# A fixed TensorE order and one head pipeline in the first layer's two attentions of a diffusion backbone

## The chip, the cores and the metric

One core of a Trainium2 chip runs the whole program. The metric is device time in microseconds (us) of one execution; less is better. PE is TensorE, DVE VectorE, ACT ScalarE, POOL GpSimd, SP SyncE; L234 is line 234 of the kernel. All data is float32.

## The reference, cut to what matters

Two layers over 512 latent and 256 context tokens of width 1024. The change touches the first sub-layer of layer 0 alone; the rest (its expert MoE, then layer 1) stays as it is.

```python
mods = split(silu(c) @ ada_w[l] + ada_b[l], 6)          # also for c_ctx: shift, scale, gate, twice
h  = rms_norm(x, norm_mix[l]) * (1 + sc1) + sh1         # hc the same from ctx
aq, ak, av, nq, nk, nv = split_cols(h @ w_in, 6 * [512])
# differential attention, 4 heads of 2 x 64: rope on aq and ak of the latents
p = softmax(q[c] . k[c] / 8)                            # c = 0, 1; keys: latents, then context
a = rms_norm((p[0] - lam * p[1]) @ v, subln) * (1 - lam_init)
# neighbourhood attention, 8 heads of 64: a window of 8 x 16 latents with a bias, and all context
nb = softmax([q . k_win / 8 + rpb, q . k_ctx / 8]) @ [v_win, v_ctx]
y = concat([a, nb]) @ w_out                             # context tokens: the same among themselves
x = x + g1 * y                                          # then the MoE of layer 0
```

## The kernel before

The kernel is written against a tile framework: it traces instructions in program order, derives all waits itself, and a scheduler then chooses each engine's order by when it takes an instruction's inputs and buffers to be ready. Only what is traced through the class Pinned (L168) keeps its place: each such TensorE instruction is tied behind the TensorE instruction traced just before it. Before the change only the MoE of layer 0 uses it.

`mix0` (L395) first makes the first third of layer 0's modulation (`ada_first`) and the normalized, transposed input `hh`, `hl` (a high and a low part, so that a product is three matmuls: `mm3`, L321). Then come twenty projection jobs (list `jobs`): per differential head a query and a key of 128 columns, two value jobs of 256, and the same for four pairs of neighbourhood heads. `proj_t` (L474) makes a query or key: 24 matmuls with 512 columns into `ps_px`, 24 with 256 into `ps_pc`; differential ones are rotated on ACT, DVE and POOL (L484 to L488). `proj_v` (L499) makes values: six groups of 24 matmuls with 256 columns, `ps_pv`. `ada` (L217) makes one of five remaining modulation vector groups: eight weight blocks of 1 MB each through two buffers, loaded by SP (L221), four 32-column matmuls per block (each is two instructions) into `ps_ada`, then transposes `ps_adat` (L244). `px`, `pc`, `pv`, `ps_ada` and `ps_adat` share two PSUM buffers.

Jobs and modulation are generators. `dense(n)` puts n jobs into the queue `fill`; `ada` generators go into `fill2`. `run_fill(n)` (L612) takes n steps of `fill` (up to the next yield), and every third turn goes to `fill2` in between; `drain` runs what is left of `fill`. A step is three or six projection matmuls, or one modulation block.

`diff_head` (L651) has six units of 128 query rows (four latent, two context). A unit is A: scores `ps_s` of both halves (64 rows of the array each, `mm3p`, L329), maximum, exponential and difference; B: up to six transposes through the single bank `ps_tr` (L687); C: the product with the values, `ps_o` (L697). `weave` (L632) runs A of a unit, then B and C of the unit before, with fill steps between, and ends each head by itself. After the last C of a head comes a chain over POOL, DVE and ACT (L703 to L710) that normalizes `au`; `tail` (L712) transposes it, called by `run_late`. `na_pair` (L734) does the same for two neighbourhood heads, scores `ps_n`, with a lag of two units; POOL adds bias and mask (L753) for DVE's L764, and the scaling is L771. During the last pair no projection is left; `last` feeds pieces of `split_wout` (L342) instead, which cast the output weights on ACT and subtract on POOL or DVE (L356). The output projection, the routing and the MoE follow.

Of the kernel before, what the change touches and what calls it, by code (L numbers as in the profile page):

```python
# [24 lines left out]
EPS = 1e-6  # L25
# [102 lines left out]

def _build(tc, a, out, dump=None, upto=99):
    nc = tc.nc  # L130
    V, S, G, T, Y = nc.vector, nc.scalar, nc.gpsimd, nc.tensor, nc.sync
    P = 128
    if dump is None:
        dump = lambda name, ap: None
# [1 line left out]
    with ExitStack() as root:  # L136
# [32 lines left out]
        class Pinned:  # L169

            @staticmethod
            def matmul(*args, **kw):
                return tc.keep_in_program_order(T.matmul(*args, **kw))  # L173

            @staticmethod
            def transpose(*args, **kw):
                return tc.keep_in_program_order(T.transpose(*args, **kw))  # L177

        garow = [dram.tile([2, 2, D], F32, name=f"garow{l}", tag=f"garow{l}") for l in range(2)]

# [36 lines left out]
        def ada(l, g, csil, wp, pp, sm):  # L217

            def load(k):
                w = wp.tile([P, 2048], F32, name="w_ada", tag="w")  # L220
                Y.dma_start(w, a["ada_w"][l, k * P:(k + 1) * P, g * 2048:(g + 1) * 2048])  # L221
                return w

            br = wp.tile([P, 512], F32, name="adab", tag="br", bufs=1)
            bsrc = a["ada_b"][l:l + 1, g * 2048:(g + 1) * 2048]
            S.dma_start(br, bass.AP(bsrc.tensor, bsrc.offset, [[512, 4], [0, 32], [1, 512]]))
            depth = 2
            ws = deque(load(k) for k in range(depth))
            yield
            ps = pp.tile([P, 512], F32, name="ps_ada", tag="mm")  # L230
            for k in range(8):
                w = ws.popleft()
                for j in range(4):
                    T.matmul(ps[32 * j:32 * j + 32, :], csil[:, k, :], w[:, j * 512:(j + 1) * 512], start=(k == 0), stop=(k == 7))  # L234
                if k + depth < 8:
                    ws.append(load(k + depth))
                yield
            row = sm.tile([P, 512], F32, name="mrow", tag="t2k", bufs=T2K)
            V.tensor_tensor(row, ps, br, op=OP.add)
            yield  # L240
            yield
            pt = pp.tile([P, 4, P], F32, name="ps_adat", tag="mm")
            for c4 in range(4):
                T.transpose(pt[:, c4, :], row[:, c4 * P:(c4 + 1) * P], ident)  # L244
            for c4 in range(4):
                src = pt[:, c4, :].rearrange("p (jh jl q) -> p jh jl q", jh=2, jl=2)[:, :, :, 0:2]
                dst = modT[l][:, 2 * g:2 * g + 2, :, c4::4].rearrange("p m v jl -> p m jl v")
                V.tensor_copy(dst, src)
            for s in range(2):
                if 1 + 3 * s in (2 * g, 2 * g + 1):  # L250
                    for v in range(2):
                        V.scalar_tensor_tensor(Asc[l][s][:, v, :], modT[l][:, 1 + 3 * s, v, :], 1.0, norm_t[:, 2 * s + l, :], op0=OP.add, op1=OP.mult)
            if g:
                for half in range(2):
                    j = 2 * (g - 1) + half
                    G.dma_start(garow[l][g - 1, :, half * 512:(half + 1) * 512], row[32 * j:32 * j + 2, :])
# [138 lines left out]
        def mix0(st, st_h, wu, stage):  # L395
# [78 lines left out]
            def proj_t(wt, dst, scale, rope):  # L474
# [2 lines left out]
                px = pp.tile([P, 512], F32, name="ps_px", tag="mm")  # L477
                for k in range(8):
                    mm3(px, wh[:, k], wl[:, k], hh[:, k, 0:512], hl[:, k, 0:512], k == 0, k == 7)
                    yield  # L480
                if rope is not None:
                    raw = sm.tile([P, 512], F32, name="raw", tag="t2k", bufs=T2K)
                    sh = sm.tile([P, 512], F32, name="sh", tag="t2k", bufs=T2K)
# [8 lines left out]
                pc = pp.tile([P, 256], F32, name="ps_pc", tag="mm")  # L492
                for k in range(8):
                    mm3(pc, wh[:, k], wl[:, k], hh[:, k, 512:768], hl[:, k, 512:768], k == 0, k == 7)
                    if k % 2:
                        yield
                split_ps(dst[:, 0, 512:768], dst[:, 1, 512:768], pc, scale)

            def proj_v(wt, dst, u):  # L499
                wh, wl = wt  # L500
                for i in range(6):
                    pv = pp.tile([P, 256], F32, name="ps_pv", tag="mm")
                    t = slice(i * P, (i + 1) * P)
                    for k in range(8):
                        mm3(pv, hh[:, k, t], hl[:, k, t], wh[:, k, :], wl[:, k, :], k == 0, k == 7)
                        if k % 2:
                            yield
                    if i % 2:
                        S.copy(dst[:, i, 256 * u:256 * u + 256], pv)
                    else:  # L510
                        V.tensor_copy(dst[:, i, 256 * u:256 * u + 256], pv)
# [30 lines left out]
            with tc.tile_pool(name="p0d", bufs=2, reuse_waits="tile") as dp:  # L542
                rope = dp.tile([P, 2, LX], F32, name="rope0", tag="rope0", bufs=1)
                with after[0], after[1], after[2]:
                    Y.dma_start(rope, a["rope0"])
                    prep(1)
                rope_of["r"] = rope
                dense(4)
                drain()
                for h in range(4):  # L550
                    dense(2)
                    for g in (((0, 1),), ((0, 2),), ((1, 0),), ((1, 1), (1, 2)))[h]:
                        fill2.append(ada(*g, csil, aw, pp, sm))
                    diff_head(h, qk["q", "d", h], qk["k", "d", h], vv, nlam, cT, pp, sm, dp)
                    drain()
                    run_late()
            for g in range(3):
                dump(f"caT{g}", cT[g][:, 0])


            dense(2)
            drain(True)
            st_a.close()
            np_ = st.enter_context(tc.tile_pool(name="p0n", bufs=2, reuse_waits="tile"))
            nv = nvt["nv"]
# [8 lines left out]
                G.memset(b[:, :, 256:512], 0.0)  # L574
            cnt = [0]

            def pair(hp):
                na_pair(hp, qk["q", "n", hp], qk["k", "n", hp], nv, nvs, bt, cnt, namask, cT, pp, sm, np_)
                drain()

            for hp in range(3):
                dense(2)
                pair(hp)

            def last(extra):
                def later():
# [2 lines left out]
                    yield from extra  # L589
                fill.append(later())  # L590
                pair(3)
                drain(True)
                for g in range(3):
                    dump(f"cnT{g}", cT[g][:, 1])
                return cT
# [36 lines left out]
        def weave(units, n_a, n_b, n_c, lag=1):  # L632

            late = deque()
            for u in list(units) + [None] * lag:
# [4 lines left out]
                if len(late) > lag:  # L640
# [4 lines left out]
                    prev[2]()  # L645
                    run_fill(n_c)

        def tr_bank(pp):
            return pp.tile([P, 4, P], F32, name="ps_tr", tag="tr", bufs=1)

        def diff_head(h, q, kk, vv, nlam, cT, pp, sm, dp):  # L651
            au = dp.tile([P, 6, P], F32, name="au", tag="au", bufs=1)
            st = dp.tile([P, 6, 8], F32, name="dst", tag="dst")

            def unit(i):
# [6 lines left out]
                def A():  # L662
                    pr = []
                    pss = [pp.tile([P, 1024], F32, name="ps_s", tag="S") for _ in range(2)]
                    for n0 in range(0, nk, 512):
                        n1 = min(n0 + 512, nk)
                        if n0:
                            run_fill(1)
                        mm3p([(pss[c][:, n0:n1], q[r, 0, qs], q[r, 1, qs], kk[r, 0, k0 + n0:k0 + n1], kk[r, 1, k0 + n0:k0 + n1]) for c, r in enumerate(HALF)])
                    for c, ps in enumerate(pss):  # L670
                        V.tensor_reduce(st[:, i, c:c + 1], ps[:, :nk], op=OP.max, axis=AX.X, negate=True)
# [4 lines left out]
                    V.scalar_tensor_tensor(st[:, i, 5:6], st[:, i, 4:5], st[:, i, 2:3], nlam[:, 3:4], op0=OP.mult, op1=OP.mult)  # L676
                    V.scalar_tensor_tensor(pr[0][:, :nk], pr[1][:, :nk], st[:, i, 5:6], pr[0][:, :nk], op0=OP.mult, op1=OP.add)
                    d["p"] = pr[0]
                    d["at"] = dp.tile([P, 6, P], F32, name="at", tag="at")

                def B(g0):
                    g1 = min(g0 + 4, n)

                    def f():
                        pt = tr_bank(pp)
                        for c in range(g0, g1):
                            T.transpose(pt[:, c - g0, :], d["p"][:, c * P:(c + 1) * P], ident)  # L687
# [4 lines left out]
                    return f  # L692

                def C():
                    po = pp.tile([P, P], F32, name="ps_o", tag="pv", bufs=1)
                    for c in range(n):
                        T.matmul(po, d["at"][:, c, :], vv[:, k0 // P + c, h * P:(h + 1) * P], start=(c == 0), stop=(c == n - 1))  # L697
                    S.copy(au[:, i, :], po)
                return A, [B(g0) for g0 in range(0, n, 4)], C

            weave([unit(i) for i in range(6)], 1, 1, 1)
            aj = dp.tile([P, 6, P], F32, name="aj", tag="at")
            G.tensor_tensor(aj, au, au, op=OP.mult)  # L703
            V.tensor_reduce(st[:, :, 6], aj, op=OP.add, axis=AX.X)

            V.scalar_tensor_tensor(st[:, :, 7], st[:, :, 2], EPS, st[:, :, 2], op0=OP.mult, op1=OP.mult)
            V.scalar_tensor_tensor(st[:, :, 6], st[:, :, 6], 1.0 / P, st[:, :, 7], op0=OP.mult, op1=OP.add)
            S.activation(st[:, :, 6], st[:, :, 6], AF.Sqrt)
            V.reciprocal(st[:, :, 6], st[:, :, 6])
            G.tensor_tensor(au, au, st[:, :, 6].unsqueeze(2).to_broadcast([P, 6, P]), op=OP.mult)  # L710

            def tail():  # L712
                yield
                for g0, g1 in ((0, 4), (4, 6)):
                    pt = tr_bank(pp)
                    for i in range(g0, g1):
                        T.transpose(pt[:, i - g0, :], au[:, i, :], ident)
                    for g in range(g0 // 2, g1 // 2):
                        V.tensor_scalar(cT[g][:, 0, h, :], pt[:, 2 * g - g0:2 * g - g0 + 2, :].rearrange("p a b -> p (a b)"), subln, None, op0=OP.mult)
                    yield  # L720
            late.append(tail())

        late = deque()

# [9 lines left out]
        def na_pair(hp, q, kk, nv, nvs, bt, cnt, namask, cT, pp, sm, np_):  # L734
# [70 lines left out]
                        S.copy(cT[2][:, 1, hp, :], po)  # L805
                return A, [B(0), B(1)], C

            weave([unit(i) for i in range(6)], 2, 1, 0, NA_LAG)

        def make_route_tiles(l):  # L810
            if l == 0:
# [997 lines left out]
```

## Time and profile before

| | |
|---|---|
| median of 3 runs | 2063.86 us (2062.2 to 2067.67) |
| the profiled execution | 2060.33 us |
| its span, first to last instruction | 2058.5 us |
| mean granted TensorE clock | 0.979 |
| PE busy | 1868.0 us (91%) |

Around the span lie 1.83 us. Busy time is the union of an engine's instructions. Matmuls are pipelined and their ends modelled, so a busy PE may still run at less than its pace; the distance from one start to the next tells what a matmul holds. Form `128*32` means a matmul with 128 rows and 32 columns of the array. The stages of the page: 0 to 69 us modulation and input, 69 to 335 differential heads, 335 to 522 neighbourhood heads, 522 to 627 output and routing, then MoE, layer 1, MoE.

### The profile page before, as it was taken

What the parts mean: (1) busy time and instruction counts of PE and PEld (TensorE: products, weight loads), DVE (VectorE), ACT (ScalarE), POOL (GpSimd) and SP (SyncE); (2) the same over time, 40 slices, a digit from 0 to 9 for tenths busy, and PEclk for the clock granted to TensorE, in tenths of its full rate; (3) what the DMA queues carried; (4) which work ended last, traced back from release to release, by engine and by line L of the source; (5) the groups of instructions that cost most, each with busy time, mean ns of one, the idle gap of its engine ahead of it and who ended that gap; (6) DMA issues with size and microseconds to landing.
All of it is one profiled execution on the core that took longest, in us unless ns stands there. A gap on an engine that the chain in (4) does not pass through costs nothing.

```text
span 2058.5 us, 25961 instructions
## 1 busy us (share of the span) xinstructions
PE 1868.0 (91%) x10612; PEld 984.2 (48%) x10612; DVE 777.8 (38%) x1703; ACT 462.3 (22%) x880; POOL 244.3 (12%) x216
## 2 busy tenths in 40 slices
PE   5899999997988999999999999999995988788787
PEld 1765556876772333333333389555582323232232
DVE  2445453456463222232313463466653112121023
ACT  3233332344330000000000242355421000000002
POOL 1201111212331000000000020101230000000000
PEclk9999999999998999999999999999997999999999
DMA  9354556213658899999999832200159999999996
GB/s 269 114 189 161 169 171 234 80 57 103 204 200 312 318 385 397 384 397 383 395 388 403 269 90 62 113 1 21 51 202 346 409 409 409 409 409 409 409 409 256
DMA packets 176463, 535.04 MB, mean 260 GB/s; under 512 B 11561, under 2 KB 51817, under 8 KB 171225
## 3 DMA queue, kind: packets, MB, share of 16 engines
q1 hardware_dynamic: 162304, 488.28, 62.8%
q0 software_dynamic: 9296, 32.68, 5.5%
q10 hardware_dynamic: 4744, 12.44, 1.9%
q8 instruction: 83, 1.36, 0.3%
q14 instruction: 36, 0.29, 0.0%
HBM read 515.76 MB, written 16.81 MB: 259 GB/s over the span
## 4 chain that ended last, share of the span: by engine, by line
PE 65%; DMA 23%; DVE 6%; ACT 2%; POOL 2%; issue 2%; SPq 0%; ACTq 0%; POOLq 0%; DVEq 0%
DMA moe_w<-in_moe_w 20%; PE ps_c L173 6%; PE ps_d L173 6%; PE ps_b L173 6%; PE ps_a L173 6%; PE ps_ada L234 3%; PE ps_px L323 3%; PE ps_px L324 2%; PE ps_px L325 2%; PE ps_e L173 2%; PE ps_s L1761 2%; PE ps_y L323 2%; PE ps_y L325 1%; PE ps_y L324 1%; PE ps_o L1784 1%
## 5 line engine op out<-in xcount | busy, mean ns | idle before, releaser
L173 PE MATMUL ps_b<-moe_w,xeT 128*64 128x512 f32 x1024 | 273.4, 597 | 31.4 <-DMA moe_w<-in_moe_w 31.4
L173 PE MATMUL ps_a<-moe_w,xeT 128*64 128x512 f32 x1024 | 275.2, 599 | 2.3 <-DMA moe_w<-in_moe_w 1.1
L173 PE MATMUL ps_d<-moe_w,hidT 128*64 128x512 f32 x1024 | 239.8, 599 | 35.5 <-DMA moe_w<-in_moe_w 35.2
L173 PEld LDWEIGHTS ps_d<-moe_w,hidT 128*64 128x64 f32 x1024 | 76.6, 137 | 193.7 <-issue 128.6
L1128 DVE TENSOR_TENSOR hid<-hid,ps_b 128x512 f32<-128x512 f32 x32 | 22.0, 687 | 379.3 <-PE ps_b L173 362.6
L173 PEld LDWEIGHTS ps_b<-moe_w,xeT 128*64 128x64 f32 x1024 | 76.1, 137 | 185.2 <-issue 131.4
L173 PEld LDWEIGHTS ps_a<-moe_w,xeT 128*64 128x64 f32 x1024 | 74.8, 137 | 135.0 <-issue 117.6
L1127 ACT ACTIVATE hid<-ps_a 128x512 f32<-128x512 f32 x32 | 19.1, 597 | 462.4 <-PE ps_a L173 462.4
L173 PE MATMUL ps_c<-moe_w,xeT 128*32 128x512 f32 x1024 | 113.2, 594 | 0.0
L1137 ACT COPY hidT<-ps_t 128x512 f32<-128x512 f32 x32 | 18.7, 586 | 313.7 <-PE ps_t L177 313.7
L1184 DVE TENSOR_SCALAR xeT<-ps_x,asc,modT 128x64 f32<-128x64 f32 (+1 forms) x256 | 64.4, 319 | 17.3 <-PE ps_x L177 16.5
L323 PE MATMUL ps_y<-woh,ch 128*128 128x512 f32 x160 | 66.0, 413 | 3.1 <-ACT ch L861 3.1
L325 PE MATMUL ps_y<-woh,cl 128*128 128x512 f32 x160 | 64.2, 401 | 0.7 <-POOL cl L862 0.7
L173 PEld LDWEIGHTS ps_c<-moe_w,xeT 128*32 128x32 f32 x1024 | 31.6, 110 | 69.0 <-issue 67.2
L324 PE MATMUL ps_y<-wol,ch 128*128 128x512 f32 x160 | 63.8, 399 | 0.0
L234 PE MATMUL ps_ada<-w_ada,csil 128*32 128x512 f32 x320 | 63.2, 604 | 0.0
L1205 DVE SCALAR_TENSOR_TENSOR ye<-ps_d,gate,g 64x512 f32<-64x512 f32 x32 | 24.0, 749 | 100.9 <-PE ps_d L173 100.6
L323 PE MATMUL ps_px<-hh,wu 128*128 128x512 f32 x128 | 58.0, 453 | 2.3 <-DVE hh L461 1.9
L1172 POOL DMA_INDIRECT xe<-gsrc,gidx x16 | 16.0, 1000 | 365.1 <-PE ps_x L177 348.2
L1333 DVE SCALAR_TENSOR_TENSOR ye<-ps_d,gate,g 128x512 f32<-128x512 f32 x14 | 10.5, 750 | 128.9 <-PE ps_d L173 128.2
L173 PE MATMUL ps_e<-moe_w,hidTc 128*32 128x512 f32 x512 | 57.9, 592 | 1.4 <-DVE yc L1216 1.4
L323 PE MATMUL ps_pv<-wh,hh 128*128 128x256 f32 x192 | 54.8, 285 | 4.6 <-DVE qk_k L319 2.3
(460 smaller groups left out, 3335.1 us busy)
## 6 DMA issues: line engine op xcount, KB each, us to landing
moe_w<-in_moe_w SPq DMA_DIRECT2D x372, 1024.0 KB
w_ada<-in_ada_w SPq DMA_DIRECT2D x40, 1024.0 KB
w_in<-in_even_w_in SPq DMA_DIRECT2D x24, 512.0 KB
w_ada<-in_ada_w SPq DMA_DIRECT2D x16, 512.0 KB
moe_w<-in_moe_w SPq DMA_DIRECT2D x16, 512.0 KB
w_in<-in_odd_w_in SPq DMA_DIRECT2D x15, 512.0 KB
w_out<-in_even_w_out SPq DMA_DIRECT2D x4, 1024.0 KB
gsrc<-xh POOLq DMA_DIRECT2D x8, 512.0 KB, 6.7
```

The source lines that it names most:

```text
L173: return tc.keep_in_program_order(T.matmul(*args, **kw))
L234: T.matmul(ps[32 * j:32 * j + 32, :], csil[:, k, :], w[:, j * 512:(j + 1) * 512], start=(k == 0), stop=(k == 7))
L323: T.matmul(ps, lh, rh, start=first, stop=False)
L324: T.matmul(ps, lh, rl, start=False, stop=False)
L325: T.matmul(ps, ll, rh, start=False, stop=last)
L1127: S.activation(hid, pa, AF.Silu)
L1128: V.tensor_tensor(hid, hid, pb, op=OP.mult)
L1137: S.copy(hT.rearrange("p (h c) t -> p c h t", h=2), pt)
L1184: V.tensor_scalar(xt[:, k, n0:n1], pt[:, c, n0:n1], Asc[0][1][:, v, k:k + 1], modT[0][:, 3, v, k:k + 1], op0=OP.mult, op1=OP.add)
L1205: V.scalar_tensor_tensor(self.ye[0:64, hs], pd[x, :], rt["gate"][x, self.e:self.e + 1], rt["g2"][x, 0, :], op0=OP.mult, op1=OP.mult)
L1761: T.matmul(ps[:, n0:n1], q[e][:, i * P:(i + 1) * P], kk[e][:, n0:n1], start=True, stop=True)
L1784: T.matmul(po[64 * e:64 * e + 64, i * P:(i + 1) * P], mv[:, c, h * 64:h * 64 + 64], d["at"][:, 6 * e + c, :], start=(c == 0), stop=(c == 5))
```

## The change

A class T takes the place of the engine's name; with T.pin set it goes through Pinned. It is set from the first projection job to the end of the last pair. All five modulation groups are queued ahead of the first four jobs. Steps are twice as long (two modulation blocks, six or twelve matmuls). Heads hand their units to one pipeline (class Pipe), which goes on from head to head; the fill step within A is gone; `au` and `at` are allocated later; a head's `tail` runs ahead of the third unit of the next head, the last head's after the values of the neighbourhood heads.

```diff
+        class T:
+            pin = False
+            @staticmethod
+            def matmul(*args, **kw):
+                return (Pinned if T.pin else nc.tensor).matmul(*args, **kw)
...
@@ ada
                 if k + depth < 8:
                     ws.append(load(k + depth))
-                yield
+                if k % 2:
+                    yield
@@ proj_t (the second product and proj_v: k % 2 becomes k % 4 == 3)
                     mm3(px, wh[:, k], wl[:, k], hh[:, k, 0:512], hl[:, k, 0:512], k == 0, k == 7)
-                    yield
+                    if k % 2:
+                        yield
@@ mix0
+                T.pin = True
+                for g in ((0, 1), (0, 2), (1, 0), (1, 1), (1, 2)):
+                    fill2.append(ada(*g, csil, aw, pp, sm))
                 dense(4)
                 drain()
+                pipe = Pipe(1, 2)
                 for h in range(4):
                     dense(2)
-                    for g in (((0, 1),), ((0, 2),), ((1, 0),), ((1, 1), (1, 2)))[h]:
-                        fill2.append(ada(*g, csil, aw, pp, sm))
-                    diff_head(h, qk["q", "d", h], qk["k", "d", h], vv, nlam, cT, pp, sm, dp)
+                    for i, u in enumerate(diff_head(h, qk["q", "d", h], qk["k", "d", h], vv, nlam, cT, pp, sm, dp)):
+                        if i == 2:
+                            run_late()
+                        pipe.push(u, 1, 1)
                     drain()
-                    run_late()
+                pipe.flush(0, 0)
...
             dense(2)
             drain(True)
+            run_late()
...
+            pipe = Pipe(2, 3)
             def pair(hp):
-                na_pair(hp, qk["q", "n", hp], qk["k", "n", hp], nv, nvs, bt, cnt, namask, cT, pp, sm, np_)
-                drain()
+                for u in na_pair(hp, qk["q", "n", hp], qk["k", "n", hp], nv, nvs, bt, cnt, namask, cT, pp, sm, np_):
+                    pipe.push(u, 0, 2)
             for hp in range(3):
                 dense(2)
                 pair(hp)
+                drain()
...
                 pair(3)
+                pipe.flush(0, 2)
                 drain(True)
+                T.pin = False
...
+        class Pipe:
+            def __init__(self, lag_b, lag_c):
+                self.lags, self.units = (lag_b, lag_c), []
+            def push(self, u, n_a, n_c):
+                self.units.append(u)
+                if u is not None:
+                    u[0]()
+                run_fill(n_a)
+                b, c = (self.units[-1 - n] if len(self.units) > n else None for n in self.lags)
+                if b is not None:
+                    b[1][0]()
+                if c is not None:
+                    c[2]()
+                if b is not None:
+                    for x in b[1][1:]:
+                        x()
+                run_fill(n_c)
+            def flush(self, n_a, n_c):
+                for _ in range(self.lags[1]):
+                    self.push(None, n_a, n_c)
@@ diff_head, A
                     for n0 in range(0, nk, 512):
                         n1 = min(n0 + 512, nk)
-                        if n0:
-                            run_fill(1)
...
-            weave([unit(i) for i in range(6)], 1, 1, 1)
+            return [unit(i) for i in range(6)]
@@ na_pair
-            weave([unit(i) for i in range(6)], 2, 1, 0, NA_LAG)
+            return [unit(i) for i in range(6)]
```

## Rows read from the trace of the kernel before

**Rows 1.** The page: engines, and the chain that ended last, by line.
```profile
PE 1868.0 (91%) x10612; PEld 984.2 (48%) x10612; DVE 777.8 (38%) x1703; ACT 462.3 (22%) x880; POOL 244.3 (12%) x216
...
DMA moe_w<-in_moe_w 20%; PE ps_c L173 6%; PE ps_d L173 6%; PE ps_b L173 6%; PE ps_a L173 6%; PE ps_ada L234 3%; PE ps_px L323 3%; PE ps_px L324 2%; PE ps_px L325 2%; PE ps_e L173 2%; PE ps_s L1761 2%; PE ps_y L323 2%; PE ps_y L325 1%; PE ps_y L324 1%; PE ps_o L1784 1%
```
**Rows 2.** Stretches: length, busy PE, PEld, DVE, ACT, POOL; granted clock, DMA share, GB/s.
```profile
69.30:117.40 48.10, 45.55 (x356) 43.02 (x354) 17.18 (x23) 11.75 (x20) 6.52 (x4) 1.00 0.23 67
117.40:335.00 217.60, 210.76 (x1255) 129.37 (x1251) 116.60 (x234) 79.77 (x177) 29.76 (x25) 0.98 0.55 182
...
384.20:488.50 104.30, 103.98 (x806) 81.30 (x804) 55.91 (x134) 40.75 (x102) 11.77 (x10) 1.00 0.15 49
488.50:522.40 33.90, 20.81 (x183) 14.59 (x181) 23.87 (x49) 16.64 (x37) 12.59 (x9) 0.90 0.36 124
```
**Rows 3.** PE in order of time: start, length, what, count; two stretches.
```profile
118.51 0.39 PE L324 MATMUL ps_px<-hl,wu 128*128 128x512 f32 x1
118.74 0.40 PE L325 MATMUL ps_px<-hh,wu 128*128 128x512 f32 x1
119.07 1.06 PE L234 MATMUL ps_ada<-w_ada,csil 128*32 128x512 f32 x8
120.06 0.50 PE L323 MATMUL ps_px<-hh,wu 128*128 128x512 f32 x1
120.40 0.39 PE L324 MATMUL ps_px<-hl,wu 128*128 128x512 f32 x1
...
121.66 1.04 PE L234 MATMUL ps_ada<-w_ada,csil 128*32 128x512 f32 x2
122.64 1.32 PE L333 MATMUL ps_s<-qk_k,qk_q 64*128 64x512 f32 x12
123.89 0.66 PE L687 MATMUL ps_tr<-ident,dp 128*128 128x128 f32 x4
...
331.86 1.90 PE L234 MATMUL ps_ada<-w_ada,csil 128*32 128x512 f32 x10
333.70 0.71 PE L697 MATMUL ps_o<-vv,at 128*128 128x128 f32 x4
```
**Rows 4.** DMA over two stretches (columns as rows 2); the one load within was issued at 175.50.
```profile
175.50 0.33 SPq L221 DMA_DIRECT2D w_ada<-in_ada_w  x1
...
177.00:179.80 2.80, 2.80 (x15) 1.52 (x15) 1.48 (x5) 0.81 (x2) 0.18 (x1) 1.00 0.80 331
179.80:181.50 1.70, 1.70 (x11) 0.79 (x11) 0.66 (x1) 0.00 (x0) 0.00 (x0) 1.00 0.00 0
```
**Rows 5.** The chain behind the first head's last unit, in order of time.
```profile
168.41 0.27 ACT L698 COPY au<-ps_o 128x128 f32<-128x128 f32 x1 [1.22 <-PE ps_o L697]
...
175.69 1.48 POOL L710 TENSOR_TENSOR au<-au,dst 128x768 f32<-128x768 f32 x1 [5.47 <-DVE dst L709]
178.66 0.88 DVE L719 TENSOR_SCALAR cT<-ps_tr,subln 128x256 f32<-128x256 f32 x2 [1.28 <-PE ps_tr L717]
```
**Rows 6.** PE waits: at a head's end, at the first value job; in total (engine <- releaser: us, times, longest).
```profile
163.75 0.68 PE L697 MATMUL ps_o<-vv,at 128*128 128x128 f32 x4 [1.83 <-DVE dst L706]
164.78 0.41 PE L325 MATMUL ps_pc<-hh,wu 128*128 128x256 f32 x1
165.00 0.41 PE L323 MATMUL ps_pc<-hh,wu 128*128 128x256 f32 x1
...
83.94 0.38 PE L323 MATMUL ps_pv<-wh,hh 128*128 128x256 f32 x1 [2.27 <-DVE qk_k L319]
...
PE ps_o L697 <- DVE dst L706: 5.5, 3, 1.8
```
**Rows 7.** DVE, then POOL, in the last pair, in order of time.
```profile
495.95 4.86 DVE L771 TENSOR_SCALAR nsp<-nsp,nst 128x512 f32<-128x512 f32 x2
501.41 0.87 DVE L771 TENSOR_SCALAR nsp<-nsp,nst 128x512 f32<-128x512 f32 x2
...
495.52 5.01 POOL L356 TENSOR_TENSOR wol<-w_out,woh 128x1024 fp32r<-128x1024 f32 x2
```

More of the change, by code (lines that the diff above doesn't have):

```diff
@@ L130, in _build @@
     nc = tc.nc
-    V, S, G, T, Y = nc.vector, nc.scalar, nc.gpsimd, nc.tensor, nc.sync
+    V, S, G, Y = nc.vector, nc.scalar, nc.gpsimd, nc.sync
     P = 128
@@ L172, in matmul, with transpose @@
             def matmul(*args, **kw):
-                return tc.keep_in_program_order(T.matmul(*args, **kw))
+                return tc.keep_in_program_order(nc.tensor.matmul(*args, **kw))
             @staticmethod
             def transpose(*args, **kw):
-                return tc.keep_in_program_order(T.transpose(*args, **kw))
+                return tc.keep_in_program_order(nc.tensor.transpose(*args, **kw))
+        class T:
[3 more added lines that the diff above has]
+                return (Pinned if T.pin else nc.tensor).matmul(*args, **kw)
+            @staticmethod
+            def transpose(*args, **kw):
+                return (Pinned if T.pin else nc.tensor).transpose(*args, **kw)
         garow = [dram.tile([2, 2, D], F32, name=f"garow{l}", tag=f"garow{l}") for l in range(2)]
@@ L494, in proj_t @@
                     mm3(pc, wh[:, k], wl[:, k], hh[:, k, 512:768], hl[:, k, 512:768], k == 0, k == 7)
-                    if k % 2:
+                    if k % 4 == 3:
                         yield
@@ L505, in proj_v @@
                         mm3(pv, hh[:, k, t], hl[:, k, t], wh[:, k, :], wl[:, k, :], k == 0, k == 7)
-                        if k % 2:
+                        if k % 4 == 3:
                             yield
@@ L651, in diff_head @@
         def diff_head(h, q, kk, vv, nlam, cT, pp, sm, dp):
-            au = dp.tile([P, 6, P], F32, name="au", tag="au", bufs=1)
+            au = []
             st = dp.tile([P, 6, 8], F32, name="dst", tag="dst")
@@ L678, in A @@
                     d["p"] = pr[0]
-                    d["at"] = dp.tile([P, 6, P], F32, name="at", tag="at")
                 def B(g0):
@@ L684, in f @@
                     def f():
+                        if g0 == 0:
+                            d["at"] = dp.tile([P, 6, P], F32, name="at", tag="at")
                         pt = tr_bank(pp)
@@ L694, in C @@
                 def C():
+                    if i == 0:
+                        au.append(dp.tile([P, 6, P], F32, name="au", tag="au", bufs=1))
                     po = pp.tile([P, P], F32, name="ps_o", tag="pv", bufs=1)
@@ L697, in C, with post @@
                         T.matmul(po, d["at"][:, c, :], vv[:, k0 // P + c, h * P:(h + 1) * P], start=(c == 0), stop=(c == n - 1))
-                    S.copy(au[:, i, :], po)
+                    S.copy(au[0][:, i, :], po)
+                    if i == 5:
+                        post()
                 return A, [B(g0) for g0 in range(0, n, 4)], C
-            weave([unit(i) for i in range(6)], 1, 1, 1)
[L702 to L710, printed above, removed]
+            def post():
+                aj = dp.tile([P, 6, P], F32, name="aj", tag="at")
+                G.tensor_tensor(aj, au[0], au[0], op=OP.mult)
+                V.tensor_reduce(st[:, :, 6], aj, op=OP.add, axis=AX.X)
+                V.scalar_tensor_tensor(st[:, :, 7], st[:, :, 2], EPS, st[:, :, 2], op0=OP.mult, op1=OP.mult)
+                V.scalar_tensor_tensor(st[:, :, 6], st[:, :, 6], 1.0 / P, st[:, :, 7], op0=OP.mult, op1=OP.add)
+                S.activation(st[:, :, 6], st[:, :, 6], AF.Sqrt)
+                V.reciprocal(st[:, :, 6], st[:, :, 6])
+                G.tensor_tensor(au[0], au[0], st[:, :, 6].unsqueeze(2).to_broadcast([P, 6, P]), op=OP.mult)
+                late.append(tail())
             def tail():
@@ L716, in tail @@
                     for i in range(g0, g1):
-                        T.transpose(pt[:, i - g0, :], au[:, i, :], ident)
+                        T.transpose(pt[:, i - g0, :], au[0][:, i, :], ident)
                     for g in range(g0 // 2, g1 // 2):
@@ L720, in tail @@
                     yield
-            late.append(tail())
+            return [unit(i) for i in range(6)]
         late = deque()
```

## The prediction

> **What bounds the kernel now.** I read the page first: PE is busy 91% of the span and no other engine half of it; the chain that ended last names PE's lines and, with 20%, transfers of the MoE's weights [rows 1]. Those are issued as the MoE frees their buffers, behind the routing, which follows the last pair; so what the touched stretches gain or lose should reach the end one for one. Next the stretches [rows 2]. While heads run, PE is busy 210.76 of 217.60 us; in pairs 0 to 2 103.98 of 104.30. Waits are small there, and a gain must come from shorter PE work. In the last pair PE is busy 20.81 of 33.90, DVE 23.87, the clock .90: nothing is full, and order decides. So I read PE's own order, by the distance from one start to the next, and what one change of work costs [rows 3]; then DMA [rows 4], the end of a head [rows 5], PE's waits [rows 6], the last pair's DVE and POOL [rows 7].
>
> **Longer modulation runs.** A run of eight `ps_ada` instructions holds PE .99 (119.07 to 120.06), one of two .98 (121.66 to 122.64), one of ten 1.84 (331.86 to 333.70) [rows 3]: a block streams once through its column groups for about .85, and a run of two pays as much as one of eight. The 40 blocks stand in 59 runs, since the scheduler cuts blocks up. Pinned, they stand in 20 runs of 16, each 1.85 by the run of ten: 59 x .985 - 20 x 1.85 = 21 less. Going into a run costs .10 (118.74 to 119.07 is .33; between plain matmuls, 118.51 to 118.74, .23), leaving it .10 (120.06 to 120.40 is .34): 39 x .20 = 8 less. Together **-29**.
>
> **Scores in one piece.** A latent unit's two 512-column products are now split by a fill step or by whatever the scheduler found. Unsplit, twelve instructions hold 1.25 (122.64 to 123.89 [rows 3]); a context unit is .55 by the same reading. Counted over the heads, `ps_s` holds 35.5 in 44 runs; in 24 whole ones 16 x 1.25 + 8 x .55 = 24.4. That is -11, and 20 changes of form less at .20, -4: **-15**.
>
> **Waits that go.** With the order fixed and lags of one and two units, C no longer follows its own B, and the value job stands behind other projection. PE's wait at the heads' last C, 5.5 in three [rows 6], goes, with the 2.27 at the first value job [rows 6]. [...] **-10**.
>
> **Waits that come, loads.** The five modulation groups are queued ahead of the first four jobs: 36 steps there bring 18 modulation turns, by my count 11 runs, 8 of them not the first of their group. In program order nothing else can go ahead of a run whose weights are not there. A load issued at 175.50 landed at 179.8, where DMA falls from .80 to 0.00 [rows 4]: 4.3; a second behind it takes some 2.5 more, as 331 GB/s at a share of .80 is about 414 when full, 1 MB. Both buffers come free as the two blocks before end, .9 apart, so the loads land about 3.4 and 5.9 after a run's end; in between stand two projection steps, 2.8. So the next run waits .6, works one block, and waits 1.5 more: 2.0 x 8 = **+16**. Bounds: 0, as the stretch now moves 67 GB/s at a DMA share of .23 [rows 2], and 4.5 x 8 = 36, if `w_in` gets between. What queues behind the waiting PE: the job's steps, then their ACT and DVE work; on SP the next modulation load waits for PE's blocks and holds the `w_in` loads traced behind it, the way from 2.0 to 4.5. Later runs have longer turns between them and wait for nothing. The biases (ACT's queue) and the vector's 4 KB bounce (POOL's queue) move ahead too, at nothing: both queues idle there.
>
> **Waits that come, tails.** Behind a head's last C stands a chain from `au`'s copy, 168.41, to the end of POOL's scaling, 175.69 + 1.48 = 177.17 [rows 5]: 8.8. Before, PE went on with projection. Now `tail` has a fixed place ahead of the next head's third unit, and between C and it stand two transposes (.2), a projection step (1.4) and on average half a modulation run (1.0): 8.8 - 2.6 = 6.2, thrice: **+18.6** (bounds 3 and 8.8 each). Its second half needs the single bank `ps_tr`, freed by two scalings of .44 with what lies around them [rows 5]: 1.1 x 4 = **+4.4**. The last head's first half is covered by value jobs. Behind the waiting PE stands A of the third unit, so the DVE and ACT work of the next units comes later by the same, nothing extra. **Clock:** after such a wait I expect what 163.75 shows, 2 each, for two of the three: **+4**. **Head starts:** the first scores of a head need the key's rotation (ACT, DVE, POOL) in program order behind its last matmul; before, other work went ahead. About 1 for three heads, **+3** (bounds 0 and 2.27 each [rows 6]).
>
> Heads and their projection: -29 - 15 - 10 + 16 + 23 + 4 + 3 = **-8**.
>
> **Pairs 0 to 2** (104.30): 52 runs of other forms become 36, both ways .3 by the price above: -4.8. B and C that lag past the third pair move into the last: -3.4. First scores of a pair wait for their key, .5 each: +1.5. **-6.5**.
>
> **The last pair** (33.90). PE needs 16.5 for what stands there and 3.4 moved in, so up to 14 are idle. DVE has 23.87 [rows 2]; it and its fill and drain, about 3 by the distance of a unit's first scores to its last C, hold 27 after: **-7** (bounds 0 and -14). DVE itself is slowed: two L771 took 4.86 beside two of POOL's subtractions (5.01), two took .87 later [rows 7]. As `split_wout` remains, I leave that as it is.
> [...]
>
> **Sum:** -8 - 6.5 - 7 = -21.5, on the profiled execution's 2060.33 (span 2058.5 and 1.83 around it): 2039. That execution lies 3.5 under the median of the runs; so by the median **2043**.
>
> **Rivals.**
> *The new waits are half covered* (.20). The chain of rows 5 holds waits of ACT and POOL that a fixed order may shorten, and a latent unit beside the loads is longer than my 2.8. Of 46 of new waits 20 stay: -21.5 - 26 = -47, **2017**. For it: DMA idles at .23 in the dense stretch [rows 2]. Against: nothing but 2.6 us of PE work stands in the tail's way.
> [...]
>
> *The gain is given back in the dense stretch* (.14): the 4.5 per run instead of 2.0, for 8 runs +20: **2063**, no change. For it: one SP queue issues both kinds of weights and stops at a load whose buffer is busy. A small part of this chance is that the order stays cut up (59 runs still, only steps longer): without the -29, -15 and +46 it would be near 2055.
>
> [...]
>
> **How the numbers follow.** A measurement of this kernel tells about 0.3% from no change: 2057.7 and 2070.0 are the bounds. The forecast (-7 to -33, 2031 to 2057) has .52, half covered .20, given back .14, slower .14. Faster: .52 + .20 = **.72**; same **.14**; slower **.14**. The range goes from 2014, the half-covered case and its own spread, to 2066, past the given-back one; the forecast's bounds (loads 0 to 36, last pair 0 to -14) lie in it. Left out are the clock case and the ends of the others, under 2 in 10.
>
> **What the profile after will show.** `ps_ada` in 20 runs of 16 and `ps_s` in 24 whole ones, else the pin does not hold. PE waiting for `w_ada` transfers ahead of the first head, about 16: near 0 makes the second case, near 36 the third. The tail's first transpose waiting for POOL's `au` three times, about 6 each, and a granted clock down behind it. [...] I am wrong altogether if the stretch to the value jobs grows, or if what is gained up to 522 is lost in the routing or the MoE.

## The result, and the profile after

The changed kernel takes 2085.31 us (median of five, 2076.58 to 2089.38) against 2063.86 for the kernel before: a ratio of 1.0091, 95% interval 1.0072 to 1.0110. It is slower by 19 to 21 us; 2043 was forecast. The profiled execution is the longest of the five, 2089.38, its span 2087.6, 29.1 more than before.

I cut the span at the same events in both traces:

| stretch | before | after | difference |
|---|---|---|---|
| start to the first head's first scores | 115.12 | 166.99 | +51.9 |
| to the first value group of the neighbourhood heads | 220.2 | 206.5 | -13.7 |
| to the end of the value groups | 48.9 | 33.9 | -15.0 |
| to the end of the last pair | 138.2 | 137.75 | -0.4 |
| output, routing, MoE of layer 0 | 648.6 | 649.9 | +1.3 |
| layer 1 and its MoE | 887.5 | 892.55 | +5.1 |

24 modulation blocks moved into the first stretch, 12 times 1.85, which is 22 of its 52; of the rest, 17 are more idle time of PE (46.9 against 30.0). The heads and values lost that work and gave back only 28.7. The last two rows are code that the change leaves alone. The traces of the eleven experiments below, with the same code there, take 1536.4 to 1540.5 from the last pair's end on; this one takes 1542.5, so most of those 6 belong to this execution.

The same columns as [rows 2], for stretches of the changed kernel:

```profile
56.57:166.99 110.42, 88.80 (x588) 59.08 (x586) 27.19 (x46) 15.88 (x24) 11.38 (x10) 0.89 0.76 259
166.99:373.51 206.52, 170.49 (x1122) 129.48 (x1119) 123.03 (x227) 77.48 (x175) 27.57 (x22) 0.89 0.30 103
373.51:407.39 33.88, 33.88 (x291) 33.88 (x290) 6.64 (x12) 5.53 (x10) 8.31 (x12) 1.00 0.41 109
407.39:545.14 137.75, 125.12 (x1016) 98.51 (x1014) 84.27 (x199) 60.98 (x147) 29.84 (x23) 0.95 0.21 71
```

Subtract busy from length: PE stands idle 21.6 us in the first, 36.0 in the heads, 12.6 in the pairs. And read the column of the granted clock: .89, .89 and .95, where [rows 2] have 1.00 and .98, and 1.00 and .90 for the pairs. PE now waits, and runs slower when it works.

Whom it waits for, in the view of waits of the changed kernel (engine, what it would write, releaser: us in all, times, longest):

```profile
PE ps_ada L173 <- DMA w_ada<-in_ada_w: 26.8, 17, 4.0
PE ps_tr L177 <- POOL au L763: 19.2, 3, 7.2
PE ps_tr L177 <- DVE nt L835: 6.4, 6, 2.8
PE ps_tr L177 <- DVE cT L773: 4.2, 4, 1.1
PE ps_tr L177 <- DVE at L738: 4.2, 6, 2.0
PE ps_n L173 <- DVE nst L818: 2.7, 1, 2.7
```

The waits that [rows 6] showed (5.5 for `dst`, 2.27 at the first value job) are gone; the six rows here make 63.5. The first of them, up to 167, where the first head starts:

```profile
PE ps_ada L173 <- DMA w_ada<-in_ada_w: 20.1, 12, 4.0
```

So 20.1 stand ahead of the first head and 6.7 within the heads. One tail shows what such a wait does. PE in order of time, then the same 20 us as stretches:

```profile
230.59 0.40 PE L173 MATMUL ps_px<-hh,wu 128*128 128x512 f32 x1
238.20 1.11 PE L177 MATMUL ps_tr<-ident,au 128*128 128x128 f32 x4 [7.21 <-POOL au L763]
240.37 0.66 PE L177 MATMUL ps_tr<-ident,au 128*128 128x128 f32 x2 [1.06 <-DVE cT L773]
240.96 2.29 PE L173 MATMUL ps_s<-qk_k,qk_q 64*128 64x512 f32 x12
243.18 1.12 PE L177 MATMUL ps_adat<-ident,mrow 128*128 128x128 f32 x4
```
```profile
229.34:234.57 5.23, 1.65 (x8) 1.02 (x7) 4.94 (x9) 2.53 (x5) 2.44 (x2) 1.00 0.00 0
234.57:244.81 10.24, 5.55 (x26) 4.33 (x27) 4.18 (x6) 2.43 (x3) 3.50 (x3) 0.50 0.00 0
244.81:250.00 5.19, 5.19 (x46) 4.97 (x47) 2.69 (x10) 2.44 (x8) 0.00 (x0) 1.00 0.01 3
```

PE stops for 7.21, the granted clock falls to .50 at 234.57, before PE goes on at 238.20, and stays there to 244.81. The unit's twelve scores hold 2.22 (240.96 to 243.18), where [rows 3] have 1.25. POOL, for which PE waits, in the same time:

```profile
233.60 1.77 POOL L500 TENSOR_TENSOR raw<-raw,rope 128x512 f32<-128x512 f32 x1 [2.65 <-DVE dst L760]
235.44 1.26 POOL L502 TENSOR_TENSOR raw<-raw,sh 128x512 f32<-128x512 f32 x1
236.66 1.48 POOL L763 TENSOR_TENSOR au<-au,dst 128x768 f32<-128x768 f32 x1
```

It rotates the next query (L500, L502) before it scales `au` (L763), though the scaling's input was made by 234.35. The second tail is the same; the third has no query to rotate there, and its wait is 4.75 instead of 7.2.

### The profile page after: what moved, and what is told of

The parts are those of the page before. It is cut to its first block, busy times and chain, and to the rows that moved or that the text cites. A ratio compares the mean times of both kernels' runs of the same rounds, so it can differ in the third digit from the quotient of the medians.

```text
span 2087.6 us, 25940 instructions
## 1 busy us (share of the span) xinstructions
PE 1853.9 (89%) x10612; PEld 994.4 (48%) x10612; DVE 784.7 (38%) x1703; ACT 460.9 (22%) x880; POOL 244.8 (12%) x216
## 4 chain that ended last, share of the span: by engine, by line
PE 63%; DMA 26%; DVE 6%; ACT 2%; issue 1%; POOL 1%; ACTq 0%; SPq 0%; POOLq 0%; DVEq 0%
DMA moe_w<-in_moe_w 19%; PE ps_c L173 7%; PE ps_a L173 6%; PE ps_d L173 6%; PE ps_b L173 6%; PE ps_y L185 4%; DMA w_ada<-in_ada_w 4%; PE ps_px L173 4%; PE ps_px L185 3%; PE ps_pv L173 2%; PE ps_e L173 2%; PE ps_s L185 2%; PE ps_pc L173 2%; PE ps_tr L177 2%; PE ps_rv L185 2%; PE ps_ada L173 2%
## 5 line engine op out<-in xcount | busy, mean ns | idle before, releaser
L173 PE MATMUL ps_px<-hh,wu 128*128 128x512 f32 x256 | 94.4, 421 | 0.0
L173 PE MATMUL ps_ada<-w_ada,csil 128*32 128x512 f32 x320 | 47.7, 691 | 26.9 <-DMA w_ada<-in_ada_w 26.8
L173 PE MATMUL ps_pv<-wh,hh 128*128 128x256 f32 x384 | 70.9, 287 | 0.0
L185 PE MATMUL ps_px<-h1h,wu 128*128 128x512 f32 (+1 forms) x224 | 63.9, 368 | 0.0
L173 PEld LDWEIGHTS ps_pv<-wh,hh 128*128 128x128 f32 x384 | 60.2, 193 | 6.1 <-issue 5.9
```

Source lines behind the costliest of these rows:

```text
L173: return tc.keep_in_program_order(nc.tensor.matmul(*args, **kw))
L185: return (Pinned if T.pin else nc.tensor).matmul(*args, **kw)
```

## The experiments

Each ran beside the kernel before on its chip; that one's medians lay between 2064.7 and 2066.7, so ratios compare better than microseconds. "Queue by head" means that modulation is queued with its head, as before the change.

**Modulation queued by head again.**

```diff
-                for g in ((0, 1), (0, 2), (1, 0), (1, 1), (1, 2)):
-                    fill2.append(ada(*g, csil, aw, pp, sm))
...
                     dense(2)
+                    for g in (((0, 1),), ((0, 2),), ((1, 0),), ((1, 1), (1, 2)))[h]:
+                        fill2.append(ada(*g, csil, aw, pp, sm))
```

> The changed kernel with one thing put back: each modulation group is queued with its head, as before the change, and not ahead of the first four jobs. Theory (a wait of PE at a fixed place costs itself and a stretch at half clock behind it): the load waits of the dense stretch (26.8 us) and the half-clock stretches there (four of 6.83 us) go, about 27 + 10, some 5 come back at the end of the queue; about 2053 us. Rival (the loads are late wherever the runs stand, so only the place of the wait moves): the waits for w_ada stay above 20 us, now within the heads, and the time stays at 2075 to 2085.

2052.38 us, ratio 0.9917 (0.9889 to 0.9945): as the theory had it. Its waits:

```profile
PE ps_ada L173 <- DMA w_ada<-in_ada_w: 8.2, 7, 3.0
PE ps_tr L177 <- POOL au L763: 7.4, 3, 2.6
PE ps_tr L177 <- DVE nt L835: 6.3, 5, 2.9
```

The loads fall from 26.8 to 8.2. The tails fall too, from 19.2 to 7.4, though nobody touched them. POOL at the first tail:

```profile
176.82 1.48 POOL L763 TENSOR_TENSOR au<-au,dst 128x768 f32<-128x768 f32 x1 [1.81 <-DVE dst L762]
178.25 1.71 POOL L500 TENSOR_TENSOR raw<-raw,rope 128x512 f32<-128x512 f32 x1
```

The scaling goes ahead of the rotation now, here and at the second tail, and from the copy of `au` to the end of the scaling it takes 5.1 (173.20 to 178.30), where the changed kernel has 9.0 (229.15 to 238.14). In one of the three tails, at 228.42, a modulation run stands in the way as well. Why the scheduler orders POOL so is not shown.

**The tail moved later.**

```diff
-                        if i == 2:
-                            run_late()
...
                 def C():
                     if i == 0:
+                        run_late()
                         au.append(dp.tile([P, 6, P], F32, name="au", tag="au", bufs=1))
```

> The changed kernel with the tail of a head moved behind the next head's third unit's scores, the fill step and its neighbour's transposes, to where the buffer au is taken again; nothing else. Theory: the three waits for POOL's au fall from 19.2 us to about 7, the half-clock stretches behind them get shorter, together 12 + 6 less: about 2067 us. Rival (what DVE and ACT do next is as late, the wait only changes its name): waits of the same size at other lines of PE, time 2080 to 2089.

2075.69, ratio 1.0038 (1.0021 to 1.0056): about half of what the theory expected, and the rival is right about the other half. The waits:

```profile
PE ps_tr L177 <- DVE at L736: 14.1, 8, 5.2
PE ps_tr L177 <- POOL au L762: 2.8, 1, 2.8
```

POOL's 19.2 become 2.8, but waits for the copy `at` grow from 4.2 to 14.1. The order on ACT and DVE says why, here for the first head's end:

```profile
238.37 0.62 ACT L326 CAST qk_q<-raw 128x512 fp32r<-128x512 f32 x1 [2.92 <-POOL raw L502]
239.02 1.30 DVE L327 TENSOR_TENSOR qk_q<-raw,qk_q 128x512 fp32r<-128x512 f32 x1 [1.05 <-ACT qk_q L326]
240.25 0.68 DVE L736 COPY at<-ps_tr 128x512 f32<-128x512 f32 x1
```

The copy stands on DVE behind the query's rotation, and that waits for ACT, which waits for POOL.

**Work in the place of the wait.**

```diff
+                    if g0 == 0 and h < 3:
+                        for _ in range(8):
+                            T.matmul(pt.rearrange("p a b -> p (a b)"), vv[:, 0, 0:P], vv[:, 0, :], start=True, stop=True)
                     for i in range(g0, g1):
                         T.transpose(pt[:, i - g0, :], au[0][:, i, :], ident)
```

> The changed kernel with eight matmuls of 512 columns added ahead of the tail's transposes of the first three heads, into the bank the transposes then overwrite; their result is not used. PE works where it waited; nothing comes earlier. Theory that the half clock behind a wait is a cost of its own: the wait turns into work of about the same length, the three 10.24 us stretches at half clock go, worth about 3.3 us each: 2075 us. Rival (the low clock is only a sign of idle time and costs nothing of its own): 2085, or more by what the eight matmuls exceed the wait.

2076.76, ratio 1.0045 (1.0033 to 1.0057): 8 to 10 less than the changed kernel, though PE does more and nothing comes earlier.

```profile
229.71 7.03 PE L173 MATMUL ps_tr<-vv 128*128 128x512 f32 x16
237.13 0.66 PE L177 MATMUL ps_tr<-ident,au 128*128 128x128 f32 x4 [0.39 <-POOL au L763]
238.84 0.41 PE L177 MATMUL ps_tr<-ident,au 128*128 128x128 f32 x2 [1.06 <-DVE cT L776]
239.18 1.32 PE L173 MATMUL ps_s<-qk_k,qk_q 64*128 64x512 f32 x12
240.43 0.66 PE L177 MATMUL ps_adat<-ident,mrow 128*128 128x128 f32 x4
```

Counted from the projection step ahead of it, the tail starts as late as without them, but the scores behind it hold 1.25 again (239.18 to 240.43). The three stretches at half clock behind the tails are gone from this trace, whose mean granted clock is .965, against .955. From the first head's first scores to the pairs' it is 6.7 shorter (235.7 against 242.4), although the third tail's matmuls hold 7 where PE had waited 4.75. So the low clock is a cost of its own, about 3 us for each: in 234.57 to 244.81 of the changed kernel PE is busy 5.55, and about half of that is lost, an estimate from the scores, which hold 2.22 there and 1.25 here.

**Pairs left to the scheduler.**

```diff
+            T.pin = False
             pipe = Pipe(2, 3)
```

> The changed kernel, with TensorE's order left to the scheduler from the first neighbourhood pair on; heads stay pinned, the pipeline and the longer steps stay. Theory: in pairs 0 to 2 the fixed order makes PE wait for DVE's and ACT's copies (6.4 us for nt, 2.7 for nst) with a half-clock stretch behind; free, the pairs 0 to 2 fall from 110.6 to about 103, and the last pair stays near 27 or goes to 30: about 2079 us. Rival (the scheduler needs its own order's buffers and the lag of two brings nothing): pairs as before the change, 138 in all, 2085.

2080.74, ratio 1.0060 (1.0038 to 1.0082); the interval overlaps the changed kernel's, so the times alone show no gain. In the trace the pairs take 130.2 (end of the values at 409.08 to 539.32) where the changed kernel has 137.75: by these two traces the pin costs there about what the pipeline gains. By the same estimate some 5 of the 7.5 are time lost at half clock that is no longer there.

**No pin, early queue kept; and no pin, queue by head.** Both leave out the line `T.pin = True`, the second has the first experiment's edit too.

> The changed kernel without the pin: TensorE's order is the scheduler's throughout, the pipeline, the longer steps and the queue ahead of the first jobs stay. Theory (what the change lost are PE's waits at fixed places, loads 27 and tails 19, with half clock behind each): both waits and the half clock go, some 60 less, and the runs are cut up again, some 30 of what the pin gained in PE work is lost: 2050 to 2060 us. Rival (the early queue itself is late, whoever orders): waits for w_ada stay over 20, time above 2070.

> The changed kernel without the pin and with the modulation queued with its head: what is left of the change is the pipeline over heads and pairs and the longer steps. Theory (the pin's fewer changes of form are worth about 30 in the heads, its waits cost about as much): 2045 to 2055, near the run with the pin and this queue (2052). Rival (fewer changes of form are worth nothing): 2035 or less, as all waits go and nothing is lost.

2041.86, ratio 0.9885 (0.9865 to 0.9905), and **2024.83**, ratio 0.9805 (0.9783 to 0.9827). Both are below what the theory expected, the second by 20 and on the rival's side: leaving the pin out costs far less PE work than I thought. What the second has from the first projection's end to the last pair's end:

```profile
69.30:113.72 44.42, 42.14 (x335) 40.80 (x333) 14.75 (x20) 8.61 (x15) 6.52 (x4) 1.00 0.25 72
113.72:306.80 193.08, 182.40 (x1253) 125.55 (x1252) 119.05 (x230) 79.67 (x178) 28.25 (x24) 0.99 0.58 204
306.80:356.59 49.79, 48.14 (x384) 38.99 (x385) 12.62 (x34) 8.32 (x15) 13.93 (x18) 1.00 0.67 209
356.59:486.10 129.51, 123.41 (x988) 96.08 (x986) 79.48 (x189) 58.47 (x142) 24.24 (x19) 0.96 0.21 72
```

The heads take 193 with the modulation in them (220 before), the pairs 129.5. The counts explain it, from PE's order over this part: how many runs, and what they hold with waits and clock in it.

```
                          ps_ada runs, us     ps_s runs, us
before                      59   60.0          44   35.5
after                       19   63.0          24   30.7
pin, queue by head          20   45.5          24   32.3
no pin, queue by head       34   47.5          25   28.2
longer steps only           41   53.2          60   41.3
```

With the queue by head the whole scores come without the pin: the pipeline has no fill step inside a unit, and the scheduler leaves the twelve matmuls together. With the early queue and no pin it does not; there `ps_s` stands in 39 runs. Of the 40 runs of `ps_ada` that the pin saves, 25 are saved without it.

**The longer steps alone; the pipeline alone; the pin without the pipeline.** The first is the kernel of before with the steps of the diff. The second is the kernel without pin and with queue by head, with the short steps of before and twice as many of them at each place. The third is the first with `T.pin` set as in the change.

> The kernel of before with the longer steps alone (two modulation blocks, six or twelve projection matmuls a step). Theory (the scheduler cuts the blocks up, a step's length hardly reaches PE): ps_ada stays near 59 runs, time within 5 of before. Rival (longer steps were what made runs of 16): fewer than 40 runs and 10 or more less than before.

> The kernel of e8_no_pin_queue_by_head with the short steps of before and twice as many of them at each place, so that the same work stands between the units: the pipeline over heads and pairs alone, no pin, queue by head. Theory (the pipeline is what gains, its units keep the scores whole and the heads' ends filled; longer steps add only the runs of ps_ada, worth about .85 each): ps_s in about 25 runs, ps_ada in 45 to 59, some 10 to 20 more than the 2025 of that run: 2035 to 2045 us. Rival (the pipeline gains only with steps that are long enough): 2055 or more.

> The kernel of before with the pin and the longer steps, and without the pipeline: modulation queued by head, each head and pair ends by itself, as e7_steps_only with the pin added. Theory (a fixed order makes PE wait wherever its next work isn't ready; the pipeline's lags cover some of it): C right behind its B and every head's and pair's end wait, 10 stops of 3 and more with half clock behind: 2110 to 2150 us, so that the pin costs more here than the 28 it costs with the pipeline. Rival (the pin pays by itself, by whole runs of ps_ada): 2055 or less.

2063.39, ratio 0.9994 (0.9978 to 1.0011): no change, though neither theory nor rival had it whole. The runs of `ps_ada` do fall to 41, but the scores, still with a fill step inside, are cut into 60, and give 5.8 of the 6.8 back. 2031.66, ratio 0.9843 (0.9829 to 0.9856): the pipeline alone holds most of the gain, 3 below the theory's range; `ps_s` in 25 runs, `ps_ada` in 43. 2151.57, ratio 1.0411 (1.0394 to 1.0429): the pin without the pipeline's lags costs 86 by the ratios, at the end of what the theory expected. Its waits:

```profile
PE ps_ada L173 <- DMA w_ada<-in_ada_w: 25.0, 17, 5.8
PE ps_tr L177 <- POOL au L726: 20.8, 4, 5.2
PE ps_tr L177 <- DVE at L705: 15.8, 7, 5.3
PE ps_tr L177 <- ACT nt L799: 13.3, 18, 2.5
```

**Edits together, and the tail once more.** First: queue by head, tail later, pairs unpinned. Second: no pin, queue by head, tail later.

> Three edits together: modulation queued with its head, the tail moved to where au is taken again, TensorE's order free from the first neighbourhood pair on. Theory (their gains are separate waits and add): the first edit alone 2052; the waits for au (7.4 there) and half clock behind them go, 5 to 8 less; the pairs 7 less: 2040 us. Rival (the pairs' 7 and the tails' gain in the runs before were the clock's chance): 2050.

> The kernel of e8_no_pin_queue_by_head with the tail at the later place. Theory (without the pin the scheduler already puts other work ahead of the tail: 3.3 us of waits for au are left): within 4 of 2025. Rival (the tail's place in the program counts without the pin too): 2015 or less.

2045.80, ratio 0.9920 (0.9896 to 0.9945): between theory and rival. The intervals don't tell it from the first experiment, so the gains were not shown to add; the waits for `at` are 10.8 in its trace, 5.0 in the first experiment's, as where the tail was moved alone. And 2023.43, ratio 0.9806 (0.9793 to 0.9820): the same as without the later tail. Without the pin a tail's place in the program made no difference that these runs can tell.

Put together, by differences of ratios at some 2065 us:

| what is varied | with what | effect on the time |
|---|---|---|
| pin | pipeline, early queue | +43 |
| pin | pipeline, queue by head | +23 |
| pin | no pipeline, queue by head | +86 |
| early queue | pin | +36 |
| early queue | no pin | +17 |
| pipeline | no pin, queue by head, longer steps | -39 |
| longer steps | no pin, pipeline | -8 |
| longer steps | no pin, no pipeline | -1, not told from 0 |

The version that beats both kernels is the change without its pin and without its early queue: 2024.83, some 40 less than before.

## Why the prediction was wrong

**What held.** `ps_ada` stands in 19 runs (two of 16 stand back to back), where 20 were forecast, a run of 16 holds 1.85, `ps_s` stands in 24 whole ones. The old waits went. The tails' waits were forecast at 18.6 and measured 19.2, their second halves 4.4 and 4.2; the first sum is partly luck. It had half a modulation run between C and a tail, and none stood there; and it took the chain from [rows 5], while two of the three tails waited for POOL's rotation.

The two traces up to the last pair's end, in three parts. What half clock costs is an estimate: half of PE's busy time at half clock, as the 256-column matmuls of before come .22 apart at .50 (164.78 to 165.00) and .12 at 1.00 (84.40 to 84.52). The forecast is split by its terms: waits of 16, 18.6, 4.4, 3 and 1.5 come, 7.8 go, and the last pair loses 7 with 3.4 of work more in it; of the -10, the 2 that are not waits are clock, beside the +4.

| | before | after | difference | forecast |
|---|---|---|---|---|
| PE idle | 53.1 | 95.5 | +42 | +25 |
| lost at half clock | 9.8 | 39.4 | +30 | +2 |
| the rest of PE's busy time | 459.5 | 410.2 | -49 | -49 |

So, by this estimate, the work that was to be saved was saved, the -29 and -15 and the -4.8 of the pairs. The clock and the waits took it back.

**The step that failed first: the clock.** "After such a wait I expect what 163.75 shows, 2 each, for two of the three: +4." This is the only term for new drops; behind loads, head starts and pairs the sum has nothing. No run shows the 2 as a term, here or in the -10. What the trace of before shows is a clock of .50 behind two of the waits at a head's last C, from 164.63 to 168.05 and from 277.27 to 280.68, with PE busy throughout; by the estimate that is 1.7 each. The changed kernel has eleven stretches at half clock of 3.41 to 10.24 in its pinned part (from 57.1 on), the kernel before three (from 69.30 on, as in [rows 2]). In all, length and busy time of each engine, changed kernel first:

```profile
sum 81.94, PE 64.64 PEld 44.12 DVE 27.65 ACT 20.07 POOL 13.85; mean PE 5.88 PEld 4.01 DVE 2.51 ACT 1.82 POOL 1.26
sum 13.65, PE 9.85 PEld 7.13 DVE 10.83 ACT 5.42 POOL 1.39; mean PE 3.28 PEld 2.38 DVE 3.61 ACT 1.81 POOL 0.46
```

Half of 64.64 is 32, against 5 before (the other 2 of the +30 lie ahead of these parts): 15 of it behind five loads, 9 behind the three tails, 2 at a head's start, 6 in the pairs. The eight idle matmuls showed the price by a run: 8 to 10 for the three tails alone. The clock case, my chance of .14 for slower, took 2 for each of 17 new stops (8 for loads, 3 tails, 3 head starts and 3 pair starts). Its 34 is close to the 32, by eleven drops of 3 and not 17 of 2; its 2073 was too low because the waits were longer too. Against it stood one wait of 2.27 with no drop behind it, at 83.94 [rows 6] in a stretch with the clock at 1.00 [rows 2]. The changed kernel has such a one as well, 2.63 for a load, ended at 126.78; but with waits of 1.39 and 1.71 close together, ended at 85.77 and 88.54, the clock fell at 87.80, and in one of 3.28, ended at 70.84, it fell at 70.73.

**The second: the loads.** "2.0 x 8 = 16" ahead of the first head, bounds 0 and 36; 20.1 were measured there, and 6.7 within the heads, where the prediction says "wait for nothing". The 4.3 of [rows 4] was a load with the queues to itself. In the first jobs some share them with the projection's weights: a load issued at 81.44 landed at 88.49, the weight behind it, issued at 81.86, at 90.12, and the DMA share from 75.00 to 95.20 was .98. Of the loads of this stretch whose landing the trace has, nine, the times are 4.7 to 7.1, the median 4.9. I had this as a bound and as the third case and left it out of the sum.

**The third: the pairs.** 13.5 was forecast for all four, 0.4 came. (The terms of pairs 0 to 2 make -6.7, not -6.5; and the 2055 that a rival gives for an order that stays cut up does not come out of its terms, which make 2040.) Cut at the end of the last projection, pairs 0 to 2 went from 103.5 to 106.5, with a wait of 2.7 for `nst` and 6.83 us at half clock in them, and the last pair from 34.7 to 31.3, half of the forecast. Unpinned, the first three take 99.2, near the 97.8 of the forecast (104.30 - 6.5). DVE's scaling in the last pair is still slowed, as in [rows 7]; DVE, then POOL:

```profile
518.36 3.60 DVE L825 TENSOR_SCALAR nsp<-nsp,nst 128x512 f32<-128x512 f32 x2
524.84 2.35 DVE L825 TENSOR_SCALAR nsp<-nsp,nst 128x512 f32<-128x512 f32 x2
527.89 0.88 DVE L825 TENSOR_SCALAR nsp<-nsp,nst 128x512 f32<-128x512 f32 x2
515.57 4.71 POOL L369 TENSOR_TENSOR wol<-w_out,woh 128x1024 fp32r<-128x1024 f32 x2 [14.79 <-ACT woh L365]
521.64 4.86 POOL L369 TENSOR_TENSOR wol<-w_out,woh 128x1024 fp32r<-128x1024 f32 x2
```

Against .88, 4.2 us are lost in two pairs of operations. POOL's subtractions stand beside both, and none beside the pair that took .88.

**The one under them.** My sum put the gains, -29 for whole modulation runs and -15 for whole scores, to the pin's account. The runs show that most of these come from the pipeline and the longer steps, with the scheduler still free, and that the pin adds waits. Two kernels, both with pipeline, longer steps and queue by head, in the parts of the table above:

| | with the pin | without it | difference |
|---|---|---|---|
| PE idle | 71.9 | 48.9 | +23 |
| lost at half clock | 29.0 | 12.1 | +17 |
| the rest of PE's busy time | 414.4 | 425.1 | -11 |

Without the pin the rest is already 34 under the 459.5 of before; the pin takes 11 more and adds 40 of waits and clock. A scheduler that may put a projection step ahead of a late transpose is a cover, and I priced its cuts but not what it hides. I named the cover of the tails, and that was the term that held.

What is still open: these parts are from one trace each, and by them the pin costs 29, by the ratios 23. The dummy matmuls were tried at the tails only, not at the loads or pairs.

## What to carry to other kernels

Before fixing an engine's order by hand, list what its scheduler hides now, for every wait that the fixed order will contain, and price the clock behind each stop as well as the stop. Split a change that reorders, regroups and fixes: here the reordering (the pipeline) was worth 39, the regrouping (longer steps) 8 on top and nothing by itself, and the fixing cost 23 to 43, without the pipeline 86. A wait that is moved may go to the next late operation on another engine's queue: look there before counting it as gained.

## What the runs showed of the hardware

A stop of PE could cost more than its length: in a wait of 7.21 the clock fell, and it stood at .50 from 234.57 to 244.81, 6.61 of it after PE went on. Filling three such waits with matmuls whose result nobody reads made the kernel 8 to 10 us faster, as that experiment had expected. Not every stop did so: the waits of 2.27 and 2.63 above left the clock as it was.
